# A gated conv-MLP with two more of its up-projection pairs per layer done in seven half products, and a new order of the products and of their weights' splits

## The chip, the cores and the metric

The kernel is one program on one core of a Trainium2 chip. The metric is the device time of one execution in microseconds (us). TensorE multiplies, ScalarE (ACT) and VectorE (DVE) work elementwise, GpSimd (POOL) issues some of the transfers, SyncE (SP) the others.

## What is computed

The reference is a decoder trunk of two layers on 512 tokens of width 1024. Layer 0 mixes tokens by a gated linear recurrence, layer 1 by an RWKV-7 recurrence. Behind each mixer stands the same channel mixer, and the change is in it alone:

```
h = rmsnorm(x, norm)
u = einsum('btd,df->btf', h, w_up)                 # 1024 -> 6144
gate = causal_dwconv(u[..., :3072], conv_w, conv_b)  # 3 taps
hid = gelu(gate) * u[..., 3072:]
x = x + einsum('btf,fd->btd', hid, w_down)         # 3072 -> 1024
```

## The kernel before

All of it is in float32. Each operand is split into two rounded parts, hi and lo (ACT casts hi, DVE subtracts to get lo), and a product is three matmuls: hi with hi, hi with lo, lo with hi (`mm3`).

The 3072 hidden columns of a channel mixer are worked off in twelve pairs, n = 0 to 11. A pair is 256 columns of the gate and the same 256 of the up part. There are two ways to do one.

- A pair of class `Whole` has four products G0, U0, G1, U1: gate or up, first or second half of the 1024 input rows. Each is 24 matmuls over 512 tokens.
- A pair of class `Halves` halves the tokens too and uses seven products instead of eight half-size ones, as Strassen and Winograd do: products 1 to 7 on sums of weights and on sums of tokens, each 24 matmuls over 256 tokens. Products 1, 6, 7 and 4 accumulate in this order into one PSUM bank (`accA`), products 5 and 3 into another (`accF`), product 2 into a third (`accD`). After 1, 6 and 7, ACT copies the bank `accA` out as it then stands, since the partial sums are needed one by one: `nc.scalar.copy(s[p], bank["A"])`, line 769. After 7, DVE adds bank `accF` to that copy (line 775).

The weights of a Halves pair are sums of blocks of `w_up`. Two of the sums are made by the transfer itself: SP fetches one block (line 166), and when it has landed POOL issues a second transfer that adds another block on top (line 168). A third sum is made by DVE (line 741), and when that one has been used, POOL adds one more block to it by a transfer (line 752), which makes the weights of product 3.

Every two pairs there is a projection down, `down`: four pieces of 24 matmuls, for pairs n - 3 and n - 2 (eight pieces, for the last four pairs, where n is 11). The program for n = 3, 5, 7, 9, 11 is: the products of pairs n - 1 and n up to product 7 of pair n; the first piece of the projection down; products 3 and 4 of pair n; the other pieces.

Pairs 3, 5, 7, 9, 11 of both layers are Halves, ten in all; pairs 0, 1, 2, 4, 6, 8, 10 are Whole. `products` runs through the list of products; `ahead` issues the splits of the weights of a Halves product two products before it is used.

What sets the order: the program is written in the order above, but a scheduler places the instructions of each engine within the limits of the data, so that TensorE can have matmuls of another product between two that depend on each other. Each engine then runs its list strictly in order. The split weights, the fetched blocks and the eight normalized inputs share one ring of 21 buffers of 4 KB for each partition (`N4`); while a channel mixer runs, 13 of them are left for weights, and a split or a fetch waits for the engine that last used its buffer.

## Time and profile before

| | |
|---|---|
| median of three runs | 1277.94 us (1277.94, 1279.1, 1277.94) |
| the profiled execution | 1279.1 us, span 1277.3 us |
| granted TensorE clock, mean | 0.998 |
| TensorE busy | 1256.0 us, 98% of the span |
| DVE, ACT, POOL busy | 929.2, 642.8, 131.1 us |
| channel mixer of layer 0 | about 155 to 541 us of the span |
| RWKV mixer | about 541 to 884 us |
| channel mixer of layer 1 | about 884 to 1250 us |

Start times are from the span's start. A matmul is listed with its modelled duration, which overlaps the next one's; what counts is the distance from start to start. In the chain that ended last, a line such as "PE accG L54 x24" is one product, and its second number is the time until the next product's start. L54, L94 and so on are lines of the kernel; `raw` is a fetched block of weights, `wh` and `wl`, `hi` and `lo` are split weights, `xs` and `xt` are the inputs and their sums, `acc` with a capital letter is a PSUM bank of an up product, plain `acc` one of the projection down.

### The profile page before, as it was taken

To read this page: it belongs to the slowest core of one execution; us is meant where nothing else is said; L and a number is where in the kernel's file an instruction comes from. 1 tells how busy PE (TensorE), PEld (TensorE's weight loads), DVE (VectorE), ACT (ScalarE), POOL (GpSimd) and SP (SyncE) were. 2 spreads that over 40 slices of the span, in tenths; PEclk is the share of its full clock that TensorE was granted. 3 is DMA by queue.
4 is the path that set the end of the run, shared out by engine and by line. 5 is a ranking of instruction groups with operands and counts; after the bars stand their busy time and mean duration, and the time that the engine had idled before them with its cause. 6 is when DMAs were issued, how large, how long until landed. Compare 5 with 4: busy or idle time off the path is not lost. (4 is left out here: it accounts for less than half of the span.)

```text
span 1277.3 us, 22409 instructions
## 1 busy us (share of the span) xinstructions
PE 1256.0 (98%) x9259; PEld 1067.4 (84%) x9259; DVE 929.2 (73%) x1412; ACT 642.8 (50%) x1006; POOL 131.1 (10%) x206
## 2 busy tenths in 40 slices
PE   9999999999999999999999898999999999999998
PEld 8777888989898989877778797778889898989896
DVE  5998678767676767789999967778776666666654
ACT  6797455434343434559845356545644334343442
POOL 3000001010101010010012145310010101000000
PEclk9999999999999999999999999999999999999999
DMA  7312335445454544413222122122345454545431
GB/s 228 109 53 97 98 119 114 158 106 167 97 175 89 181 83 137 141 57 110 67 75 68 35 63 85 50 94 83 127 88 181 83 182 83 182 83 182 98 133 66
DMA packets 117829, 141.37 MB, mean 111 GB/s; under 512 B 10138, under 2 KB 91748, under 8 KB 117600
## 3 DMA queue, kind: packets, MB, share of 16 engines
q1 hardware_dynamic: 100528, 122.44, 29.9%
q0 software_dynamic: 16624, 16.47, 8.3%
q8 instruction: 72, 1.18, 0.4%
q10 hardware_dynamic: 576, 1.05, 0.2%
q14 instruction: 29, 0.24, 0.1%
HBM read 135.41 MB, written 4.52 MB: 110 GB/s over the span
## 5 line engine op out<-in xcount | busy, mean ns | idle before, releaser
L97 DVE TENSOR_TENSOR wl<-raw,wh 128x1024 fp32r<-128x1024 f32 (+1 forms) x161 | 194.4, 1213 | 123.6 <-ACT wh L94 103.8
L94 ACT CAST wh<-raw 128x1024 fp32r<-128x1024 f32 (+1 forms) x161 | 165.9, 1043 | 179.8 <-PE acc L54 40.7
L54 PE MATMUL accU<-xs,wh 128*128 128x512 f32 x448 | 138.6, 391 | 0.0
L54 PE MATMUL accG<-xs,wh 128*128 128x512 f32 x448 | 138.6, 390 | 0.0
L54 PE MATMUL acc<-hid,wh 128*128 128x512 f32 x384 | 117.9, 389 | 0.0
L748 DVE TENSOR_TENSOR lo<-raw,hi 128x1024 fp32r<-128x1024 f32 x70 | 85.5, 1222 | 39.4 <-PE accU L54 32.0
L747 ACT CAST hi<-raw 128x1024 fp32r<-128x1024 f32 x70 | 73.7, 1054 | 60.4 <-PE accU L54 25.3
L54 PEld LDWEIGHTS accU<-xs,wh 128*128 128x128 f32 x448 | 83.7, 188 | 17.1
L54 PEld LDWEIGHTS accG<-xs,wh 128*128 128x128 f32 x448 | 83.7, 188 | 17.0
L54 PE MATMUL accU<-xs,wl 128*128 128x512 f32 x224 | 87.2, 389 | 0.0
L54 PE MATMUL accG<-xs,wl 128*128 128x512 f32 x224 | 87.2, 389 | 0.0
L54 PE MATMUL accA<-xt,hi 128*128 128x256 f32 x480 | 83.5, 277 | 0.0
L54 PEld LDWEIGHTS acc<-hid,wh 128*128 128x128 f32 x384 | 71.4, 188 | 14.3
L54 PE MATMUL acc<-xs,wh 128*128 128x512 f32 x256 | 80.9, 398 | 0.0
L694 DVE SCALAR_TENSOR_TENSOR cv<-gpad,pv,cv 128x512 f32<-128x512 f32 x96 | 69.1, 747 | 13.1 <-ACT cv L692 12.7
L848 PE MATMUL acc<-wh,hid 128*128 128x512 f32 (+1 forms) x200 | 76.2, 381 | 0.0
L849 PE MATMUL acc<-wl,hid 128*128 128x512 f32 (+1 forms) x200 | 76.1, 381 | 0.0
L847 PE MATMUL acc<-wh,hid 128*128 128x512 f32 (+1 forms) x200 | 76.1, 381 | 0.0
L54 PE MATMUL acc<-hid,wl 128*128 128x512 f32 x192 | 74.3, 389 | 0.0
L168 POOL DMA_DIRECT2D raw<-in_ffn_w_up_dram x20 | 25.7, 1285 | 469.8 <-DVE x L863 166.5
L54 PEld LDWEIGHTS accA<-xt,hi 128*128 128x128 f32 x480 | 72.6, 188 | 0.0
L54 PE MATMUL accA<-xt,lo 128*128 128x256 f32 x240 | 66.3, 276 | 0.0
(411 smaller groups left out, 2938.0 us busy)
## 6 DMA issues: line engine op xcount, KB each, us to landing
raw<-in_ffn_w_up_dram SPq DMA_DIRECT2D x106, 512.0 KB, 3.9
raw<-in_ffn_w_down_dram SPq DMA_DIRECT2D x48, 512.0 KB, 4.0
raw<-in_ffn_w_up_dram POOLq DMA_DIRECT2D x30, 512.0 KB, 5.7
raw<-in_rwkv_w_rkv_dram SPq DMA_DIRECT2D x24, 512.0 KB, 3.8
raw<-in_lru_w_in_dram SPq DMA_DIRECT2D x16, 512.0 KB, 4.0
raw<-in_lru_w_out_dram SPq DMA_DIRECT2D x8, 512.0 KB, 3.8
raw<-in_rwkv_w_out_dram SPq DMA_DIRECT2D x8, 512.0 KB, 3.8
xd<-x SPq DMA_DIRECT2D x8, 256.0 KB, 2.1
```

What stands on the lines that cost most here:

```text
L54: mm = lambda *a, **kw: self.nc.tensor.matmul(ps, *a, skip_group_check=more, **kw)
L94: put = (self.nc.vector.tensor_copy if dve else self.nc.scalar.copy)(hi, src)
L97: self.nc.vector.tensor_tensor(lo, src, hi.bitcast(F32), ALU.subtract)
L168: self.nc.gpsimd.dma_start(raw, more, accum_op=ALU.add)
L694: nc.vector.scalar_tensor_tensor(cv, pair.gp[:, e, j : j + T], cw(j), cv, ALU.mult, ALU.add)
L747: nc.scalar.copy(hi, f[p])
L748: tt(lo, f[p], hi.bitcast(F32), ALU.subtract)
L847: nc.tensor.matmul(ps, hh[:, s], wh[:, k, m], start=kk == 0, stop=False)
L848: nc.tensor.matmul(ps, hl[:, s], wh[:, k, m], start=False, stop=False)
L849: nc.tensor.matmul(ps, hh[:, s], wl[:, k, m], start=False, stop=kk == blocks - 1)
```

## The change

Pairs 6 and 10 of both layers become Halves, so that 14 of the 24 pairs are. The order of a Halves pair's products goes from 1, 5, 6, 2, 7, 3, 4 to 1, 2, 5, 6, 7, 3, 4, and the order in which its blocks are fetched follows. A new limit `cap` holds back the splits for the next pair while the projection down runs, until `prepare` lifts it in the second half of the projection; the fetches for a Halves pair that follows stand in the middle of the projection down (`fetch`), or, for an odd pair, behind the first product or product 5 of the pair before. The splits of the projection's weights are asked for after product 7 of odd pairs alone.

```
-HALVES = (3, 5, 7, 9, 11)
+HALVES = (3, 5, 6, 7, 9, 10, 11)
...
-for first, more in (((0, 0), None), ((1, 1), (1, 0)), ((0, 1), None), ((1, 0), (0, 0)), ((1, 1), None)):
+for first, more in (((0, 0), None), ((0, 1), None), ((1, 1), (1, 0)), ((1, 0), (0, 0)), ((1, 1), None)):
...
-order = ((1, 5, 6, 2, 7), (3, 4))
+order = ((1, 2, 5, 6, 7), (3, 4))
...
-    pair.f = dict(zip((1, 5, 2, 7), [self.loaded.pop(i + j) for j in range(4)]))
+    pair.f = dict(zip((1, 2, 5, 7), [self.loaded.pop(i + j) for j in range(4)]))
...
-    nc.gpsimd.dma_start(f[3], self.plan[i + 2][0], accum_op=ALU.add)
+    nc.gpsimd.dma_start(f[3], self.plan[i + 1][0], accum_op=ALU.add)
...
-    while made[0] < min(j, len(seq)):
+    while made[0] < min(j, cap[0]):
...
-    if p == "G0" and n + 1 in HALVES:
+    if p in ("G0", 5) and n % 2 == 0 and n + 1 in HALVES:
         self.weights_load(quads[n + 1] + 4)
...
-    if p == 7:
+    if p == 7 and n % 2:
         self.weights_split(behind[n] + 2)
...
+def fetch(n):
+    if n in HALVES:
+        self.weights_load(quads[n] + 4)
+def prepare():
+    cap[0] = len(seq)
+    ahead(at[0] + 2)
...
     products((n, 7))
+    cap[0] = seq.index((n, 4)) + 1
...
-    down(n, 2 * n - 6, 4 if n < 11 else 8, lambda: products((n, 4)), lambda: ahead(at[0] + 2))
+    down(n, 2 * n - 6, 4 if n < 11 else 8, lambda: products((n, 4)), lambda: fetch(n + 1), prepare)
```

What the scheduler made of it shows on TensorE between products 6 and 7. Both accumulate into `accA`. In pair 3 of layer 0, before, product 6 (weights `lo_2022`) was followed by product 2 into `accD`:

```order
L54 MATMUL accA<-xt,lo_2022 128x256
L54 MATMUL accA<-xt,hi_2021 128x256 x2
L54 MATMUL accA<-xt,lo_2022 128x256
L54 MATMUL accD<-xs_1412,hi_2053 128x256 x2
L54 MATMUL accD<-xs_1412,lo_2054 128x256
```

Now product 6 (`hi_2052`) is followed by four matmuls of the projection down (`acc_2189`), and then by product 7 (`hi_2086`):

```order
L54 MATMUL accA<-xt,hi_2052 128x256 x2
L54 MATMUL accA<-xt,lo_2053 128x256
L54 MATMUL acc_2189<-hid,wh_2179 128x512 x2
L54 MATMUL acc_2189<-hid,wl_2180 128x512
L54 MATMUL acc_2189<-hid,wh_2179 128x512
L54 MATMUL accA<-xt,hi_2086 128x256 x2
L54 MATMUL accA<-xt,lo_2087 128x256
```

So the 24 matmuls of product 2 that stood between the two writers of `accA` have become four of another kind. In the new Halves pair 6 the place between 6 (`hi_2960`) and 7 (`hi_2994`) holds two matmuls, the first of product 1 of pair 7:

```order
L54 MATMUL accA<-xt,hi_2960 128x256 x2
L54 MATMUL accA<-xt,lo_2961 128x256
L54 MATMUL accA<-xs_1262,hi_3095 128x256 x2
L54 MATMUL accA<-xt,hi_2994 128x256 x2
L54 MATMUL accA<-xt,lo_2995 128x256
```

Before, pair 6 was Whole, and its second and third products went into two different banks, one behind the other:

```order
L54 MATMUL accU<-xs_1317,wh_2920 128x512 x2
L54 MATMUL accU<-xs_1317,wl_2921 128x512
L54 MATMUL accG<-xs_1412,wh_2962 128x512 x2
L54 MATMUL accG<-xs_1412,wl_2963 128x512
L54 MATMUL accG<-xs_1431,wh_2962 128x512 x2
```

In pair 7, which follows a Halves pair, product 7 (`hi_3238`) stands directly behind product 6 (`hi_3204`); pair 11 behind pair 10 is the same, and layer 1 repeats all of it:

```order
L54 MATMUL accA<-xt,lo_3205 128x256
L54 MATMUL accA<-xt,hi_3204 128x256 x2
L54 MATMUL accA<-xt,lo_3205 128x256
L54 MATMUL accA<-xt,hi_3238 128x256 x2
L54 MATMUL accA<-xt,lo_3239 128x256
```

On ACT, in the pair 5 of before, the three copies out of `accA` (L769) stood with one or two casts between them:

```order
L769 COPY s<-accA 128x512
L747 CAST hi_2673<-raw_2610 128x1024
L769 COPY s<-accA 128x512
L94 CAST wh_2707<-raw_2705 128x1024
L94 CAST wh_2713<-raw_2711 128x1024
L769 COPY s<-accA 128x512
```

In the pair 6 of after, three casts stand between the copy behind product 1 and the one behind product 6: those of products 3 and 4 (`hi_3033`, `hi_3063`) and that of product 1 of the next pair (`hi_3095`):

```order
L769 COPY s<-accA 128x512
L747 CAST hi_3033<-raw_2850 128x1024
L747 CAST hi_3063<-raw_2992 128x1024
L747 CAST hi_3095<-raw_3023 128x1024
L769 COPY s<-accA 128x512
L747 CAST hi_3125<-raw_3025 128x1024
L769 COPY s<-accA 128x512
```

The copy that product 7 waits for has thus moved behind the cast of a weight block that pair 7 uses.

More of the change, by code (lines that the diff above doesn't have):

```diff
@@ L797, in ffn @@
             seq = [(n, p) for n in range(12) for part in kind(n).order for p in part]
-            made, at = [0], [0]
+            made, at, cap = [0], [0], [len(seq)]
             def ahead(j):
-                while made[0] < min(j, len(seq)):
+                while made[0] < min(j, cap[0]):
                     n, p = seq[made[0]]
@@ L824, in products, with down @@
                         return
-            def down(n, b0, blocks, between, then):
+            def down(n, b0, blocks, between, then, soon):
                 final = n == 11
@@ L854, in down @@
                                             finish(b, m, xtok[:, b, :], pool)
+                                if g and b == 1:
+                                    soon()
                             if not g and cs[0] == 0:
@@ L871, in hook @@
                                 then()
+                            elif g and c == pieces - 2:
+                                soon()
                         self.project(hids, ev, kb=blocks, join=2 if g else 1, rate=0.5 if final else 2, after=hook, x0=b0)
```

## The prediction

> **What bounds the kernel now.** I read the busy times first, then the chain of work that ended last, then a table by stage, and last the engines' own rows around one Halves pair.
>
> ```profile
> PE 1256.0 (98%) x9259; PEld 1067.4 (84%) x9259; DVE 929.2 (73%) x1412; ACT 642.8 (50%) x1006; POOL 131.1 (10%) x206
> ```
>
> TensorE works through 98% of the span. A busy PE is not always PE at its pace, so I look at the chain in the channel mixer of layer 1, where each line is one product and its second number the time to the next start:
>
> ```profile
> 933.53 5.44 PE accG L54 x24
> 938.97 5.44 PE accU L54 x24
> 944.41 5.44 PE accG L54 x24
> 949.85 5.44 PE accU L54 x24
> 955.29 2.87 PE accA L54 x24
> 958.16 2.74 PE accF L54 x24
> 960.90 2.72 PE accA L54 x24
> 963.62 2.86 PE accD L54 x24
> 966.48 2.74 PE accA L54 x24
> ...
> 974.68 2.87 PE accF L54 x24
> 977.55 2.74 PE accA L54 x24
> ...
> 1144.57 2.87 PE accA L54 x24
> ```
>
> A Whole pair is four lines of 5.44 us, 21.76 us. A Halves pair is seven, 2.87 + 2.74 + 2.72 + 2.86 + 2.74 + 2.87 + 2.74 = 19.54 us. One line begins where the last one ends: TensorE waits for nothing here. The table shows one period of two pairs with its projection down, for layers 1 and 0 (columns: busy us of PE, weight load, DVE, ACT, POOL, then clock, DMA share, GB/s):
>
> ```profile
> 955.29:1018.38 63.09, 63.09 (x362) 55.59 (x362) 39.86 (x47) 25.25 (x31) 3.82 (x3) 1.00 0.50 134
> 284.00:347.00 63.00, 63.00 (x361) 55.50 (x361) 41.60 (x52) 25.05 (x30) 3.81 (x3) 1.00 0.50 134
> ```
>
> DVE is idle for a third, ACT for more than half. So matmuls taken away shorten the time directly, and any wait on TensorE lengthens it directly.
>
> **The gain.** Four pairs go from 21.76 to 19.54 us: 4 x 2.22 = 8.9 us less.
>
> **The extra work beside it.** Each of these pairs gets three more casts on ACT and three more subtractions and one sum on DVE, three copies out of PSUM, and some 512-wide DVE operations. How densely these follow each other is in these rows:
>
> ```profile
> 203.46 1.21 DVE L748 TENSOR_TENSOR lo<-raw,hi 128x1024 fp32r<-128x1024 f32 x1
> 204.60 0.68 DVE L97 TENSOR_TENSOR hid<-s,hid 128x512 fp32r<-128x512 f32 x1
> 205.20 0.68 DVE L726 TENSOR_TENSOR s<-s,ge 128x512 f32<-128x512 f32 x1
> ```
>
> A wide DVE operation takes a slot of 1.14 us, a narrow one 0.60. Four wide ones and about three narrow ones are 6.4 us of DVE; with 39.9 to 41.6 in the table that is 46 to 48 of the 60.8 us that a period of two Halves pairs would last (2 x 19.54 + 4 x 5.44). ACT goes to about 30. Neither becomes the bound by its sum. SP gets one more fetch per pair, POOL three adding transfers where a Whole pair had none. Held-back splits (`cap`) and the earlier fetch cost nothing by themselves: the blocks of pair 6 are asked for once the first down piece has freed their buffers, some 17 us before they are used (two products and three pieces, 5.6 + 3 x 5.44 = 21.9 us, less a fetch of 3.9 and its cast); if that cover were gone, product 1 would wait.
>
> **The new wait, bare.** The old order had product 2 between 6 and 7; now 7 follows 6 at once. Both write bank `accA`, and 7 may not start before ACT has copied the bank. What such a copy costs is in these rows:
>
> ```profile
> 1146.72 1.05 ACT L747 CAST hi<-raw 128x1024 fp32r<-128x1024 f32 x1 [0.70 <-DVE lo L748]
> 1147.68 0.58 ACT L769 COPY s<-accA 128x512 f32<-128x512 f32 x1
> 1147.81 1.23 DVE L748 TENSOR_TENSOR lo<-raw,hi 128x1024 fp32r<-128x1024 f32 x1 [0.52 <-ACT hi L747]
> ...
> 1152.74 0.39 PE L54 MATMUL accD<-xs,hi 128*128 128x256 f32 x2
> 1152.94 0.59 ACT L769 COPY s<-accA 128x512 f32<-128x512 f32 x1 [3.73 <-PE accA L54]
> 1153.82 1.05 ACT L94 CAST wh<-raw 128x1024 fp32r<-128x1024 f32 x1 [0.29 <-DMA raw<-in_ffn_w_down_dram]
> 1154.89 1.23 DVE L97 TENSOR_TENSOR wl<-raw,wh 128x1024 fp32r<-128x1024 f32 x1 [4.43 <-ACT wh L94]
> ```
>
> The copy begins 0.20 us after the next product's first matmul and takes 0.59. An ACT cast lets the next instruction start after 0.96 us; DVE starts 0.04 us after the cast it needs. For the step from ACT to TensorE I take the nearest case, in the RWKV mixer:
>
> ```profile
> 639.84 1.05 ACT L94 CAST wh<-raw 128x1024 fp32r<-128x1024 f32 x1
> 640.93 0.50 PE L54 MATMUL acc<-mix,wh 128*128 128x512 f32 x1 [1.57 <-ACT wh L94]
> ```
>
> The cast ends at 640.89, the matmul starts 0.04 later and takes 0.50 instead of the usual 0.39, so 0.11 us more for a weight load that nothing hides. A bare gap is 0.20 + 0.59 + 0.04 + 0.11 = 0.94 us. The 0.11 may not arise, since here the weights were what was waited for; I take it and keep 0.83 as the lower end. On that point the Trainium skill (TensorE: Matmul & The Clock Gate, "Step-by-step: what each phase is for") says that weight loads are pulled ahead of matmuls in flight; by that rule each bare gap would be 0.83, and the sum below 0.9 us lower. The row here is of the other kind and can't decide it.
>
> **Where it is paid, pair by pair.**
>
> Pairs 3, 5 and 9 (six in two layers) follow a Whole pair. Four down matmuls stand in the gap, 4 x 5.44/24 = 0.91 us. They need the down weights early: their `lo` part was ready 11.55 us after product 1 of its pair (1154.89 + 1.23 less 1144.57), and the third of the four is due at 11.19 + 0.45 = 11.64 us. That just fits, since the fetch still waits for the second product. I book 0.05 each, 0.3 in all; nothing to 0.4 each are the ends.
>
> Pairs 7 and 11 (four) have nothing in the gap: 0.94 each, 3.8 in all, if ACT is free. Ahead of that copy ACT has two gelus, a cast and two casts of the hidden block, which I count to end 0.4 to 0.6 us early.
>
> Pairs 6 and 10 (four) have two matmuls, 0.24 us, but ACT is late there. I count from product 1 of pair 6: products end at 2.87, 5.73, 8.47 and 11.19 (1, 2, 5, 6). The ring of buffers orders the rest: `hi` of product 3 takes the buffer of the last product but one, `lo` of 3 and `hi` of 4 those of product 5, and the cast for pair 7 waits for `lo` of 4. So `lo` of 3 starts on DVE at 8.6 and holds it to 9.75, `lo` of 4 ends at 9.76 + 1.22 = 10.98, the cast for pair 7 runs from 11.02, and the copy of product 6 behind it starts at 11.98 and ends at 12.57. Product 7 starts at 12.57 + 0.04 + 0.11 = 12.72 instead of 11.43: 1.3 us. In layer 1, DVE adds the last down block before it splits product 6's weights (0.2 + 0.7 + 1.2 us after the pair's start), so POOL starts the transfer for product 3 at 2.1:
>
> ```profile
> L168 POOL DMA_DIRECT2D raw<-in_ffn_w_up_dram x20: 1258/1276/1378, 196.9 to 1188.9; - x20
> ...
> DMA to landing us min/median/max: 5.6/5.7/7.5
> ...
> L752 POOL DMA_DIRECT2D raw<-in_ffn_w_up_dram x10: 1261/1277/1301, 214.8 to 1200.1; - x10
> ...
> DMA to landing us min/median/max: 5.6/5.7/6.4
> ...
> raw<-in_ffn_w_up_dram SPq DMA_DIRECT2D x106, 512.0 KB, 3.9
> ```
>
> It lands at 7.85, the cast of product 3 ends at 8.9, and the same chain gives 13.1: 1.7 us. Two such pairs in each layer: 2 x 1.3 + 2 x 1.7 = 6.0 us.
>
> Behind product 7 of these four pairs stand six matmuls of pair 7, then ten of product 4, then product 3. Product 4 waits for the copy of 7 (0.20 + 0.59 after its end, against 0.72 of cover); product 3 waits for DVE, which first splits a block whose buffer product 7 frees, then adds bank F: 0.20 + 1.14 + 0.69 against 0.72 + 0.07 + 1.14 of cover. I book 0.2 each, 0.8 in all; 0 to 0.5 each are the ends.
>
> **The sum.** -8.9 + 0.3 + 3.8 + 6.0 + 0.8 = +2.0 us. Against the profiled execution (1279.1 us, 1.2 above the median) that is 1281.1; against the median, 1279.9. The RWKV mixer's instructions are also placed a little differently, since the scheduler sees another start, and TensorE has idle time there:
>
> ```profile
> 541.00:884.00 343.00, 331.33 (x4282) 272.50 (x4281) 284.94 (x521) 197.77 (x386) 73.60 (x142) 1.00 0.23 71
> ```
>
> Of 343.0 us it is busy for 331.3; I allow an eighth of the 11.7 idle, 1.5 us either way. A difference under 0.2% (2.6 us) can't be told from none here. With all lower ends (0.83 bare, nothing for the six and the 0.8, even pairs without the 0.11) the sum is -8.9 + 3.3 + 5.6 = 0.0, with all upper ones +2.0 + 2.1 + 1.2 = +5.3.
>
> **The rivals.**
>
> *The gaps are mostly covered.* The scheduler put two matmuls into the gaps of pairs 6 and 10, as if the copy were on time; if the buffers came free earlier than I count, those gaps would cost 0.94 - 0.24 = 0.7 us, the 0.8 would go, and the sum would be -8.9 + 0.3 + 3.8 + 2.8 = -2.0, with gaps of 0.83 about -2.9: 1275.0 to 1276. Against it: the chain from the end of product 5 (cast, subtraction, cast, copy) is made of durations above and has no slack.
>
> *A transfer comes late, and the kernel is clearly slower.* POOL adds the second block for product 5 of pair 7 once SP's fetch has landed. SP issues that at about 3.5 (behind product 1's buffers and two fetches), it lands 3.9 later, and 5.7 more make 13.1 to 14. On DVE the sum that needs it stands ahead of the addition of bank F that product 3 of pair 6 waits for. The split between the two starts when product 7 has ended (15.4 + 0.2), so with a slot of 1.14 for the sum the transfer may land at 14.4 at the latest; at the 7.5 us of the slowest adding transfer it lands at 15 to 16, about 1.2 us late in each of four pairs: +2.0 + 4.8 = +6.8, 1284.7. For it speaks that eight transfers of 512 KB meet in 20 us there; against it that most took 5.7.
>
> *The clock drops.* After a gap the chip once granted half the clock (columns: busy us of PE, clock, DMA share, GB/s), though not after the gap at 640.93:
>
> ```profile
> 793.50:794.00 0.50, 0.00 (x0) 1.00 1.05 426
> ...
> 796.50:797.00 0.50, 0.17 (x4) 0.82 0.00 0
> 797.50:798.00 0.50, 0.50 (x13) 0.50 0.12 33
> ...
> 799.50:800.00 0.50, 0.50 (x17) 0.50 1.13 135
> 800.00:800.50 0.50, 0.50 (x5) 0.76 0.71 102
> ...
> 640.00:645.00 5.00, 4.07 (x17) 3.06 (x18) 4.83 (x11) 2.79 (x3) 0.00 (x0) 1.00 0.16 61
> ```
>
> That is some 3.4 us at half speed, 1.7 us lost. Four even pairs with that would add 6.8 us: 1286.7. TensorE had little work from 793.5 to 796.9; my gaps are 1.3 us between dense products, shorter than the harmless one of 1.57. The Trainium skill warns of it in the same page ("A second HAM failure mode: psum-queue depth-cycling"): short idle times between matmul groups can make the clock swing. Its table asks for no idle gap over about 3 us ("Why this matters for your kernels"), which the quoted gap at 640.93 agrees with.
>
> **How the numbers follow.** My sum holds with 60%, the covered gaps with 17%, the late transfer with 17%, the clock with 6%. In my own case a little under two thirds lies within 0.2% and the rest above. Faster by over 0.2% comes from the covered gaps: 12%. Slower: 17 + 6 + 20 = 43%. The same: 45%. The range from 1275.8 to 1285.0 takes in the covered gaps, all ends of my terms and the late transfer, and leaves out the clock and a part of each tail. My own case by itself is 1278 to 1283.
>
> **What would show it.** Right: in the chain of the changed kernel the products of a Halves pair keep 2.72 to 2.87 us, and TensorE shows idle time ended by the copy at line 769, about 0.9 us in pairs 7 and 11 and 1.3 to 1.7 in 6 and 10. Periods of pairs 6 and 7 with their projection take 60.8 us plus about 2.5. Wrong: no idle time before product 7; or idle time before product 3 of pair 6 that ends with DVE, which had waited for an adding transfer; or a clock under 1.00 in these stretches; or a change in the RWKV mixer larger than 1.5 us.

## The result, and the profile after

The changed kernel takes 1313.79 us (median of four, 1313.4 to 1314.05), against 1278.18 before: 1.0275 times as long, 95% interval 1.0263 to 1.0287. The prediction had 1279.9 us, 1275.8 to 1285.0 as its range. It was wrong by 34 us.

The first lines of the page of the changed kernel, busy times and the fetches of `w_up`:

```profile
PE 1260.8 (96%) x9547; PEld 1080.3 (82%) x9547; DVE 954.5 (73%) x1440; ACT 657.9 (50%) x1030; POOL 146.3 (11%) x218
...
raw<-in_ffn_w_up_dram SPq DMA_DIRECT2D x110, 512.0 KB, 3.8
...
raw<-in_ffn_w_up_dram POOLq DMA_DIRECT2D x42, 512.0 KB, 5.8
```

DVE and ACT have hardly more to do than before, and the median landing times, 3.8 and 5.8 us, are near the 3.9 and 5.7 of before. Nothing here explains 34 us. The waits of TensorE do (engine and operation, what released it: us in total, times, longest):

```profile
PE accA L54 <- ACT hi L747: 12.9, 4, 6.3
PE accF L54 <- DVE s L775: 6.0, 2, 3.6
PE acc L54 <- ACT wh L94: 4.5, 3, 2.2
PE accA L54 <- ACT s L769: 4.4, 4, 1.5
```

The wait that I had booked, on the copy at line 769, is the last of the four. The two above all are on a cast (747) and on the addition of bank F (775). Where they lie is seen by stage: first the couple of pairs 6 and 7 with its projection in the kernel before, and the stretch from the rest of the last projection of layer 0 to layer 1; then the same in the changed kernel, with the couples 10/11 up to product 4 of pair 11. Columns as in the prediction's table.

```profile
327.21:390.30 63.09, 63.09 (x361) 55.59 (x360) 41.70 (x51) 25.07 (x30) 3.81 (x3) 1.00 0.50 134
500.15:884.08 383.93, 372.26 (x4462) 306.27 (x4461) 319.78 (x566) 220.91 (x417) 73.60 (x142) 1.00 0.25 77
```

```profile
328.42:397.30 68.88, 63.68 (x434) 58.96 (x432) 44.36 (x56) 28.23 (x35) 5.09 (x4) 0.98 0.60 161
460.72:511.44 50.72, 45.85 (x362) 43.94 (x361) 30.97 (x38) 18.97 (x24) 5.09 (x4) 1.00 0.71 171
511.44:902.54 391.10, 373.35 (x4463) 306.13 (x4462) 325.11 (x570) 223.14 (x419) 73.47 (x142) 1.00 0.24 76
1078.67:1150.12 71.45, 63.97 (x433) 59.65 (x432) 43.29 (x52) 28.38 (x36) 6.47 (x5) 0.95 0.62 160
1213.63:1266.89 53.26, 47.45 (x362) 45.94 (x360) 30.53 (x34) 21.17 (x27) 5.71 (x5) 0.94 0.69 179
```

With nothing lost, a couple 6/7 would last 63.09 - 2.22 = 60.87 us, a couple 10/11 up to there 46.76 - 2.22 = 44.54 (the 46.76 is the same piece of before). So the four couples of two Halves pairs lose 8.0 and 6.2 us in layer 0, 10.6 and 8.7 in layer 1, 33.5 together. I call this the loss of a couple below. The account of the spans (1311.9 against 1277.3, 34.6 more): -8.9 gained, +33.5 in the couples, +2.0 in the six odd Halves pairs behind a Whole (0.30 to 0.41 each), +7.2 in the stretch to layer 1 (391.10 against 383.93), +0.8 in small shifts at both ends. The sum of the prediction was +2.0.

**What happens in layer 1, pair 6.** The adding transfer for product 3 and the four plain fetches for pair 7, each by its line:

```profile
L752 POOL DMA_DIRECT2D raw<-in_ffn_w_up_dram x1: 1283/1283/1283, 1081.6 to 1081.6; - x1
...
DMA to landing us min/median/max: 9.9/9.9/9.9
```

```profile
L166 SPq DMA_DIRECT2D raw<-in_ffn_w_up_dram x4: 367/408/892, 1081.6 to 1084.5; - x4
...
DMA to landing us min/median/max: 4.1/9.6/10.0
```

At 1081.6, three us into pair 6, POOL starts the add for product 3 (line 752) and SP, in the next three us, the four plain fetches for pair 7. From 1086 to 1091 us the DMA engines are full (share 1.10). The add lands after 9.9 us instead of 5.7; the first fetch still lands after 4.1 us, the others after up to 10.0 instead of 3.9. Now the order of the lists, on ACT and on TensorE:

```profile
1091.56 1.99 ACT L747 CAST hi<-raw 128x1024 fp32r<-128x1024 f32 x2 [9.23 <-DMA raw<-in_ffn_w_up_dram]
1095.21 1.04 ACT L747 CAST hi<-raw 128x1024 fp32r<-128x1024 f32 x1 [1.66 <-DVE lo L748]
1096.16 0.58 ACT L769 COPY s<-accA 128x512 f32<-128x512 f32 x1
...
1096.31 0.80 PE L54 MATMUL accA<-xs,hi 128*128 128x256 f32 x2 [6.26 <-ACT hi L747]
```

ACT stands 9.23 us at the cast for product 3, which waits for the add. Behind it stand the cast for product 4, the first cast for pair 7 and the copy of bank A. TensorE has two matmuls of pair 7's product 1 ahead of product 7 and waits 6.26 us for their weights, and all of this for a product 3 that is not due yet.

**What happens in layer 0.** Here POOL starts the add for product 3 earlier, and it lands in 5.9 us. The adds for pair 7 are late (DVE's list and the matmul that waited for it):

```profile
346.89 1.23 DVE L741 TENSOR_TENSOR raw<-raw,raw 128x1024 f32<-128x1024 f32 x1 [4.96 <-DMA raw<-in_ffn_w_up_dram]
348.03 1.22 DVE L748 TENSOR_TENSOR lo<-raw,hi 128x1024 fp32r<-128x1024 f32 x1
349.16 0.68 DVE L775 TENSOR_TENSOR s<-s,accF 128x512 f32<-128x512 f32 x1
...
349.90 0.71 PE L54 MATMUL accF<-xs,hi 128*128 128x256 f32 x2 [3.59 <-DVE s L775]
```

That is the prediction's second rival as it stands there: the sum at 741 stands ahead of the addition of bank F. Only it ends 3.6 us late instead of 1.2.

**And the clock.** Stretches of half a microsecond (the last three columns are clock, DMA share, GB/s), the first behind a wait of 2.43 us, the others in and behind longer ones:

```profile
481.00:481.50 0.50, 0.46 (x4) 0.47 (x5) 0.50 (x1) 0.00 (x0) 0.00 (x0) 1.00 0.00 0
350.50:351.00 0.50, 0.50 (x4) 0.50 (x4) 0.50 (x2) 0.00 (x0) 0.00 (x0) 0.50 0.00 0
1094.00:1094.50 0.50, 0.00 (x0) 0.00 (x0) 0.50 (x1) 0.00 (x0) 0.50 (x1) 0.63 0.01 4
1227.00:1227.50 0.50, 0.00 (x0) 0.00 (x0) 0.41 (x2) 0.04 (x1) 0.16 (x1) 0.75 0.44 137
```

Behind three of the four waits TensorE runs at half the clock for a while. In layer 0 product 3 takes 4.47 us from start to start instead of 2.87, so 1.6 us of the 8.0 are the clock. In layer 1 TensorE worked at half the clock for 4.6 and 4.3 us behind the two waits, which by the same reckoning makes about 2.3 us of the 10.6 and 2.1 of the 8.7 (an estimate from the clock's changes in the trace).

### The profile page after: what moved, and what is told of

Its sections match the earlier page's. It is cut to its first block, busy times and chain, and to the rows that moved or that the text cites. A ratio compares the mean times of both kernels' runs of the same rounds, so it can differ in the third digit from the quotient of the medians.

```text
span 1311.9 us, 23103 instructions
## 1 busy us (share of the span) xinstructions
PE 1260.8 (96%) x9547; PEld 1080.3 (82%) x9547; DVE 954.5 (73%) x1440; ACT 657.9 (50%) x1030; POOL 146.3 (11%) x218
## 3 DMA queue, kind: packets, MB, share of 16 engines
q0 software_dynamic: 22960, 22.76, 11.2%
## 4 chain that ended last, share of the span: by engine, by line
PE 37%; DVE 7%; ACT 4%; issue 2%; DMA 2%; POOL 1%; SPq 0%; POOLq 0%; ACTq 0%; DVEq 0%
PE acc L54 6%; PE accA L54 4%; PE accU L54 4%; PE accG L54 4%; PE acc L849 3%; PE acc L847 3%; PE acc L848 3%; PE accF L54 2%; DMA raw<-in_ffn_w_up_dram 2%; DVE X L1323 1%; DVE wl L97 1%; PE accD L54 1%; DVE DA L1321 1%; PE s L1437 1%; DMA raw<-in_ffn_w_down_dram 1%
## 5 line engine op out<-in xcount | busy, mean ns | idle before, releaser
L747 ACT CAST hi<-raw 128x1024 fp32r<-128x1024 f32 x98 | 102.6, 1050 | 143.4 <-DMA raw<-in_ffn_w_up_dram 39.8
L748 DVE TENSOR_TENSOR lo<-raw,hi 128x1024 fp32r<-128x1024 f32 x98 | 119.6, 1222 | 66.4 <-ACT hi L747 35.7
L54 PE MATMUL accA<-xt,hi 128*128 128x256 f32 x672 | 122.3, 284 | 4.4 <-ACT s L769 4.4
L54 PEld LDWEIGHTS accA<-xt,hi 128*128 128x128 f32 x672 | 105.2, 193 | 6.8 <-ACT s L769 6.3
L54 PE MATMUL accU<-xs,wh 128*128 128x512 f32 x320 | 99.2, 391 | 0.0
L54 PE MATMUL accG<-xs,wh 128*128 128x512 f32 x320 | 99.2, 391 | 0.0
L54 PE MATMUL accA<-xt,lo 128*128 128x256 f32 x336 | 94.5, 281 | 0.0
L54 PEld LDWEIGHTS accU<-xs,wh 128*128 128x128 f32 x320 | 59.6, 188 | 12.1
L54 PEld LDWEIGHTS accA<-xt,lo 128*128 128x128 f32 x336 | 64.9, 193 | 0.0
L54 PE MATMUL accU<-xs,wl 128*128 128x512 f32 x160 | 62.4, 390 | 0.0
```

The source lines that it names most:

```text
L54: mm = lambda *a, **kw: self.nc.tensor.matmul(ps, *a, skip_group_check=more, **kw)
L747: nc.scalar.copy(hi, f[p])
L748: tt(lo, f[p], hi.bitcast(F32), ALU.subtract)
```

## The experiments

Theory A: transfers that meet land late, and TensorE waits for them through the order of ACT's and DVE's lists. Theory B: the new order of products and the place of instructions cost it, the transfers little. This table sums up all runs. Losses are of the couples, in us, from TensorE's start times in each trace; the last column is the stretch from the rest of layer 0's last projection to layer 1. In e3 the even pairs begin up to 2.6 us inside the projection ahead, which counts as loss here, and its trace is of its slowest execution (1321.6 us).

| run | median us | 6/7, 10/11 of layer 0 | 6/7, 10/11 of layer 1 | sum | stretch |
|---|---|---|---|---|---|
| before | 1278 | - | - | - | 383.9 |
| changed | 1313.8 | 8.0, 6.2 | 10.6, 8.7 | 33.5 | 391.1 |
| e1 ten pairs | 1282.9 | - | - | - | 383.4 |
| e2 old order | 1295.7 | 4.9, 7.6 | 4.5, 3.9 | 20.8 | 388.1 |
| e3 kernel before, fourteen pairs | 1314.9 | 10.0, 10.1 | 14.2, 11.9 | 46.2 | 393.3 |
| e4 half of the couples' adds left out | 1295.7 | 2.7, 4.2 | 2.9, 3.6 | 13.4 | 391.3 |
| e5 plain instead of adds | 1301.1 | 3.6, 3.7 | 7.1, 4.3 | 18.8 | 391.6 |
| e6 no add for 3 | 1301.6 | 3.9, 4.5 | 8.3, 6.0 | 22.7 | 390.7 |
| e7 pair 10 Whole | 1293.1 | 8.5, - | 9.9, - | 18.4 | 381.5 |
| e8 sums on DVE, old order | 1289.0 | 3.2, 3.2 | 1.9, 1.8 | 10.2 | 391.5 |
| e9 DVE order | 1335.3 | 10.5, 8.4 | 15.8, 15.7 | 50.4 | 393.8 |
| e10 DVE order, no add for 3 | 1323.9 | 10.7, 9.1 | 11.5, 9.8 | 41.0 | 393.7 |
| e11 e8, pair 10 of layer 0 Whole | 1278.0 | 3.2, - | 1.9, 1.8 | 6.9 | 381.7 |
| e12 e11, product 1 earlier | 1277.1 | 2.5, - | 1.8, 1.8 | 6.1 | 381.8 |
| e13 ACT order | 1314.1 | 3.4, 7.6 | 10.4, 11.2 | 32.6 | 391.8 |
| e14 all three orders | 1305.9 | 8.7, 4.3 | 7.0, 4.9 | 25.0 | 391.8 |
| e15 e12, layer 1 alone | 1278.0 | - | 1.8, 1.8 | 3.6 | 382.2 |

**e1: the ten old pairs with all other edits.**

```
-HALVES = (3, 5, 6, 7, 9, 10, 11)
+HALVES = (3, 5, 7, 9, 11)
```

> The changed kernel with the old ten Halves pairs (3, 5, 7, 9, 11 in each layer) and every other edit kept: the new product order, the later splits, the earlier fetch. No Halves pair follows another here. Theory A (transfers that meet): four fetches and one adding transfer fall into some 5 us after the start of pairs 6 and 10, land after 6.5 to 10 us instead of 3.9 and 5.7, and TensorE waits for them through the order of ACT and DVE; without pairs 6 and 10 that is gone, and what is left is the new order after a Whole pair, 0.3 us in each of ten pairs as the chain of the changed kernel shows for pairs 3, 5 and 9: 1278.2 + 3 = 1281 us. Theory B (the new order itself and where ACT and DVE instructions stand): then this kernel should lose much of it too, 1290 us or more. The 7.2 us that the stretch from the last projection of layer 0 to the start of layer 1 lost: if they come with the edits of fetch and splits they are here too, and the time is about 1288; if they come from pairs 10 and 11, they are gone.

1282.93 us, 1.0031 times before (1.0020 to 1.0043). The edits without the couples cost 5 us: 4.0 in the ten pairs (0.17 to 0.52 each), most of the rest ahead of the first of them. The stretch to layer 1 is as before. So the time goes where two Halves pairs stand side by side.

**e2: the old order of products, fourteen pairs.**

```
-order = ((1, 2, 5, 6, 7), (3, 4))
+order = ((1, 5, 6, 2, 7), (3, 4))
```

> The changed kernel with fourteen Halves pairs, but the products in the old order 1, 5, 6, 2, 7 (and the blocks of a pair asked for in the old order). Theory A: the same transfers meet in the same 5 us, and the block for product 5 of pair 7 is needed even earlier; the gaps before product 7 are covered by product 2, so about 4 x 1.4 + 6 x 0.3 = 7 us go, but most of the 25 us of waits on transfers stays: 1300 to 1312 us. Theory B: with the order the loss goes too, and the gain of 8.9 us shows: below 1280 us.

1295.74 us, ratio 1.0129 (1.0112 to 1.0145): below A's range, far above B's. The order is worth 12.7 us in the couples, 2.0 in the six odd pairs, which lose nothing here, and 3.0 in the stretch; 20.8 stay in the couples with it. So Theory B has a large part too.

**e3: the kernel before with fourteen pairs and little else.**

```
-HALVES = (3, 5, 7, 9, 11)
+HALVES = (3, 5, 6, 7, 9, 10, 11)
...
-    if p == 7:
+    if p == 7 and n % 2:
```

> The kernel before with fourteen Halves pairs and nothing else of the change (splits for the projection down asked for after product 7 of odd pairs alone, as they must be): old order, no early fetch of a pair behind a Halves pair, so the blocks of pairs 7 and 11 are asked for only when the weights of their product 1 are prepared. Theory A: the fetches come together and later than in the changed kernel, so the waits are as long or longer: 1310 us or more. Theory B: the old order has no gap, so the gain of 8.9 us shows in part: 1270 to 1280 us.

1314.9 us (1311.05 to 1321.63), ratio 1.0288 (1.0252 to 1.0323), as A had it. The old order alone does not carry fourteen pairs.

**e4: without three of the six adding transfers of each couple,** those behind which TensorE was seen to wait. The adds for products 5 and 7 of pairs 6 and 10 and for product 3 of pairs 7 and 11 stay.

```
-plan.append((a(*first), 4, True, more and a(*more)))
+plan.append((a(*first), 4, True, more and n not in (7, 11) and a(*more) or None))
...
-if p == 6:
+if p == 6 and pair.n % 2:
     nc.gpsimd.dma_start(f[3], self.plan[i + 1][0], accum_op=ALU.add)
```

> The changed kernel without the adding transfers in the couples 6/7 and 10/11: the second block is not added for products 5 and 7 of pairs 7 and 11, nor for product 3 of pairs 6 and 10 (so those weights are incomplete); every fetch, cast, sum and product stays. Theory A: no cast and no sum waits for an adding transfer, and the plain fetches land sooner. The gap before product 7 of pairs 6 and 10 falls from 1.1 to 6.4 us to about 1, the wait before product 3 (3.6 and 2.4 us) and the half clock go; the four couples lose about 2.4 to 3 us each instead of 6.2 to 10.6: 1313.8 - 33.5 + 11 = about 1291 us. Theory B: the waits are set by buffers and by the order on ACT and DVE, with the transfers only last in line by little: less than 8 us go, 1306 us or more.

1295.74 us, ratio 1.0137 (1.0118 to 1.0155); the couples lose 13.4. Its waits:

```profile
PE accA L54 <- ACT s L769: 5.2, 4, 2.1
PE acc L54 <- ACT wh L94: 4.5, 3, 2.2
PE accA L54 <- ACT hi L747: 3.8, 4, 0.9
```

The wait on bank F is gone, that on the cast is 0.9 us at most. Twenty of the 33.5 us hang on these adding transfers. What is left, 13.4, is near the 10.6 that the prediction had for the couples (3.8 + 6.0 + 0.8).

**e5: the same transfers, plain.**

```
-self.nc.gpsimd.dma_start(raw, more, accum_op=ALU.add)
+self.nc.gpsimd.dma_start(raw, more)
...
-nc.gpsimd.dma_start(f[3], self.plan[i + 1][0], accum_op=ALU.add)
+nc.gpsimd.dma_start(f[3], self.plan[i + 1][0])
```

> The changed kernel with every adding transfer of POOL turned into a plain one of the same block at the same place (it overwrites instead of adding, so these weights are incomplete). Number, bytes, queue and order of the transfers stay. Theory A1 (adding is what is slow: with an adding transfer under way the DMA engines are full at 165 to 200 GB/s, without one they move 300 to 385): the plain ones land after about 4 us also when they meet others, and the couples fall to near the kernel without adds, 13 to 18 us lost instead of 33.5: 1293 to 1299 us. Theory A2 (too many transfers at once, whatever they do): the five that meet still land after 6 to 10 us, and the time stays above 1308 us.

1301.05 us, ratio 1.0172 (1.0157 to 1.0188), couples 18.8: between the two, nearer A1. The transfer for product 3 in pair 6 of layer 1, which took 9.9 us as an add:

```profile
L752 POOL DMA_DIRECT2D raw<-in_ffn_w_up_dram x1: 760/760/760, 1077.3 to 1077.3; - x1
...
DMA to landing us min/median/max: 7.3/7.3/7.3
```

In layer 0, where it starts 1.5 us ahead of the fetches, the plain one took 4.2. So both count: of the 20 us that the adds cost, 14.7 go when the adding goes, and about 5.4 (18.8 less 13.4) when the transfers go too. The split is rough, since this edit takes the adding from all six transfers of a couple and e4 leaves three of them.

**e6: no add for product 3 in pairs 6 and 10.** The second edit of e4 alone.

> The changed kernel without the adding transfer for product 3 of the even Halves pairs (6 and 10) alone; those of pairs 7 and 11 stay (so product 3's weights of pairs 6 and 10 are incomplete). If the gap of 4.8 to 6.3 us before product 7 in layer 1 comes from this transfer alone (it took 8.8 and 9.9 us to land, and ACT's next casts stood behind the cast that waited for it), it falls to about 1 us with the half clock behind it: 10 to 12 us less. In layer 0 the waits of 3.6 and 2.4 us before product 3 come from the adds for pairs 7 and 11; they stay, or lose 1 to 2 us with the lighter traffic. In all 1298 to 1304 us. Rival: with the gap gone, TensorE in layer 1 reaches product 3 earlier and waits there for the sum behind the adds of pair 7, as layer 0 does: only 5 to 7 us less, 1306 to 1309 us.

1301.57 us, ratio 1.0169 (1.0149 to 1.0189). The wait before product 7 of the even pairs falls to 0.95 us in layer 1 too, as expected; the rival came true beside it:

```profile
PE accF L54 <- DVE s L775: 7.5, 4, 3.0
```

Layer 1 now waits before product 3, which it did not before. In layer 0 that wait fell from 3.6 and 2.4 to 1.0, since the lighter traffic let the adds for pair 7 land sooner.

**e7: pair 10 a Whole pair.** `HALVES = (3, 5, 6, 7, 9, 11)`.

> The changed kernel with pair 10 as a Whole pair again (twelve Halves pairs: 3, 5, 6, 7, 9, 11). By the account of the changed kernel's chain the two couples 6/7 stay at 8.0 and 10.6 us of loss, the couples 10/11 lose nothing, eight odd pairs behind a Whole cost 0.3 each: 1278 - 4.4 + 18.6 + 2.5 + 0.8 = 1295.5 us, if the 7.2 us lost between the last products of layer 0 and the start of layer 1 come from the couple 10/11 that ends layer 0. If they come from a state that the couple 6/7 or the whole layer leaves, they stay: 1303 us.

1293.06 us, ratio 1.0106 (1.0091 to 1.0121). The couples 6/7 lose 8.5 and 9.9, close to the 8.0 and 10.6 of the changed kernel, and the stretch to layer 1 is back at 381.5: its 7.2 us come from the couple that ends layer 0.

**e8: sums on DVE in place of every adding transfer, old order.** The second blocks are in the buffers anyway, as blocks of other products; the blocks are fetched for products 1, 5, 7, 2 and 3 in turn.

```
+if p == 5:
+    tt(f[5], f[5], f[7], ALU.add)
+    tt(f[7], f[7], f[1], ALU.add)
 if p == 6:
     tt(f[1], f[5], f[1], ALU.add)
...
+if p == 2:
+    tt(f[3], f[3], f[2], ALU.add)
```

> Fourteen Halves pairs in the old product order, and no adding transfer at all: the blocks are fetched plainly and added by DVE out of blocks that are in the buffers anyway (product 5's from the blocks for 5 and 7, product 7's from those of 7 and 1, product 3's from those of 6 and 2). Everything is computed. DVE pays three sums of 1.14 us a pair. Theory A: with no add to wait for and with the gap before product 7 covered by product 2, the couples lose about 1 to 2 us each; 1278 - 8.9 + 6 + 4 to 7 in the mixer = 1279 to 1282 us, under 1278 if the mixer's loss goes too. Rival: DVE, at 46 to 48 of 60.8 us in a couple plus 6.8 for the sums, now comes late itself, and the splits behind the sums make TensorE wait: 1290 us or more.

1288.97 us, ratio 1.0078 (1.0061 to 1.0095), above what A gave, though the couples lose only 10.2; the longest wait of TensorE in them is 0.8 us. I had the mixer wrong again: the stretch is at 391.5, 7.6 more than before.

**e9: the late sum held back on DVE.**

```
+with tc.issue_after(mark[0].ins):   # product 3's addition, pair 6 or 10
     pairs[n].weights(p)             # p = 5, 6 of pair 7 or 11
```

> The changed kernel, all transfers as they are, with one thing held on DVE: the splits and the sum for products 5 and 6 of pairs 7 and 11, which need the late block, are queued behind product 3's addition of the pair before, as the program text has them (the scheduler had put the sum ahead of the addition of bank F). Theory: in layer 0 TensorE's wait of 3.6 and 2.4 us before product 3 is the order on DVE alone, since the product that needs the late block comes 9 us later; it goes, with the half clock behind it, and the couples of layer 0 fall from 8.0 and 6.2 us to about 2.7 and 4.2 (what is left without adds). In layer 1 the wait before product 7 stands behind product 3's add and stays: 10.6 and 8.7. In all 7.3 us less: 1306 to 1307 us. Rival: the late block is late for pair 7 itself, and the wait only moves on to its products 5 or 6: less than 3 us gained, 1311 us or more.

1335.27 us, ratio 1.0445 (1.0430 to 1.0461): 21 us worse than the changed kernel. The wait before product 3 did go. But the sum now ran at 352.4 instead of 346.9, the add of pair 7's own product 3 started later and met the fetches for the projection down, and ACT and TensorE show the next place:

```profile
365.56 1.04 ACT L747 CAST hi<-raw 128x1024 fp32r<-128x1024 f32 x1 [5.72 <-DMA raw<-in_ffn_w_up_dram]
366.51 0.58 ACT L769 COPY s<-accA 128x512 f32<-128x512 f32 x1
...
367.14 0.80 PE L54 MATMUL accA<-xt,hi 128*128 128x256 f32 x2 [5.90 <-ACT s L769]
```

The same pattern as in pair 6 of layer 1, now in pair 7: a cast that waits for an add stands ahead of the copy of bank A. My theory that the order on DVE alone was at fault in layer 0 fell with this.

**e10: the same without the add for product 3 of pairs 6 and 10.**

> The same, and the adding transfer for product 3 of pairs 6 and 10 left out as well (so product 3's weights of these pairs are incomplete); the adds for pairs 7 and 11 stay. If the two waits, on product 3's add through ACT and on the sum that stands ahead on DVE, are the whole of what the adding transfers cost, the four couples lose what they lose without any adds, 13.4 us together instead of 33.5: 1293 to 1296 us. If there is a third cost of the adds for pairs 7 and 11, the couples stay above 18 us: 1299 us or more.

1323.92 us, ratio 1.0355 (1.0340 to 1.0371). There is a third cost, and it is that of e9: the waits before product 7 of the odd pairs, 4.6 to 7.0 us, stay. The changed kernel does not have it, its waits there are 0.7 to 1.5 us, so it came with the order held on DVE.

**e11: e8 with pair 10 of layer 0 Whole.**

> The kernel of the DVE sums in the old order, with pair 10 of layer 0 a Whole pair again (thirteen Halves pairs). The stretch from the last products of layer 0 to layer 1 took 391 us in every kernel whose pairs 10 and 11 are both Halves there, 381 to 384 where pair 10 is Whole. If that is the cause, this kernel loses 3.2 us of its couple less, gains 2.2 less, and gets 7 to 10 us back in the mixer: 1289.0 - 1.0 - 8 = about 1280 us. Rival: the mixer's time hangs on the whole order ahead of it in no simple way, and stays near 391: 1288 us.

1278.0 us, ratio 0.9993 (0.9984 to 1.0003). Eleven us less than e8, more than I expected, nearly all of it in the stretch to layer 1 (e8, then e11):

```profile
502.85:894.37 391.52, 372.15 (x4462) 304.62 (x4461) 326.11 (x571) 223.17 (x419) 74.30 (x142) 1.00 0.24 76
```

```profile
501.19:882.93 381.74, 370.87 (x4462) 304.88 (x4461) 319.81 (x566) 220.86 (x417) 74.99 (x142) 1.00 0.24 77
```

TensorE has the same 4462 matmuls and DVE five instructions more in e8; TensorE idles 19.4 us in e8 and 10.9 in e11.

**e12: e11, with product 1 of pairs 7 and 11 ahead of products 3 and 4 of the pair before.**

> As the last one, and product 1 of pairs 7 and 11 stands between product 7 and products 3 and 4 of the pair before it, so that the copy of bank A and the addition of bank F have 2.9 us of matmuls beside them. The gaps of 0.44 us and what goes with them (0.1 for the reload) in three couples go: 1 to 2 us below the last kernel, 1278 to 1279 us. Rival: the next pair's weights are then needed 5 us earlier, and the splits and sums for them are late: 1283 us or more.

1277.08 us, ratio 0.9991 (0.9982 to 1.0001). The couple of layer 0 loses 2.5 instead of 3.2, those of layer 1 no more than in e11, so the rival did not come true.

**e13: the cast for product 3 held back on ACT, in pairs 6 and 10.**

```
+with tc.issue_after(mark[6].ins):   # the copy after product 6
     pairs[n].weights(p)             # p = 3
```

> The changed kernel, all transfers as they are, with one thing held on ACT: the cast for product 3 of pairs 6 and 10, which waits for the adding transfer, is queued behind the copy of bank A after product 6 instead of ahead of it and of pair 7's first cast. If the 4.8 and 6.3 us before product 7 in layer 1 are the order on ACT alone (product 3 itself is due 3.4 us later and could still meet its block), they fall to about 1 us with the half clock behind them, and the couples of layer 1 fall from 10.6 and 8.7 to about 4 us: 1302 us. If the run of dependent transfers is late as a whole (block for product 3 landed, then the fetches and adds for pair 7), the wait moves to the next instruction that hangs on it, product 4 or 3 of the same pair, as it moved when the sum was held back on DVE: 3 us gained or less in each couple of layer 1, none in layer 0: 1307 to 1313 us.

1314.13 us, ratio 1.0283 (1.0266 to 1.0300): no change in all. (The edit also asks for the weights of product 3 one product later.) The wait before product 7 of pair 6 in layer 1 is 0.67 us now, and pair 7 has this:

```profile
1115.83 0.80 PE L54 MATMUL accA<-xt,hi 128*128 128x256 f32 x2 [6.37 <-ACT s L769]
```

Against what I expected, layer 0 changed too: couple 6/7 fell from 8.0 to 3.4, its wait on bank F gone, and couple 10/11 rose from 6.2 to 7.6.

**e14: all three places mended at once,** e9 and e13 together, e13's also for pairs 7 and 11.

> The changed kernel, all transfers as they are, with both held orders together and on both pairs of a couple: on DVE the splits and the sum for products 5 and 6 of pairs 7 and 11 behind product 3's addition of the pair before, on ACT the cast for product 3 behind the copy of product 6, in pairs 6, 7, 10 and 11. These are the three places at which TensorE was seen to wait behind an instruction that waits for an adding transfer. If the cost of the adds is order alone, it is gone now, and the couples lose about 3 to 4 us each: 1294 to 1300 us. If the blocks are late for the pair's work itself, the wait has a fourth place to go to (the casts of the weights for the projection down, which stand behind the cast for product 3 of pairs 7 and 11) and the time stays above 1308 us.

1305.93 us, ratio 1.0211 (1.0192 to 1.0230), couples 25.0. Between the two: these three orders gain 8.5 of the 20 us and not the other 11.6. But order is not used up by them. In layer 0 TensorE now waits one copy later, before product 4 of pair 7, and the half clock comes with it (from 366.5 to 373.3 us):

```profile
364.59 1.99 ACT L747 CAST hi<-raw 128x1024 fp32r<-128x1024 f32 x2 [3.32 <-DMA raw<-in_ffn_w_up_dram]
366.49 0.58 ACT L769 COPY s<-accA 128x512 f32<-128x512 f32 x1
...
367.12 0.80 PE L54 MATMUL accA<-xt,hi 128*128 128x256 f32 x2 [2.79 <-ACT s L769]
```

The cast for product 3, which waits for its add, stands ahead of the copy after product 7 here. So how the 11.6 us part between late data and order that is left stays open.

**e15: even Halves pairs in layer 1 alone,** otherwise e12.

> DVE sums in place of the adding transfers, old order, product 1 of the next pair ahead of products 3 and 4, and even Halves pairs in layer 1 alone (twelve Halves pairs in all). In the run with pair 6 of layer 0 as well, the couple there lost 2.5 us against 2.2 gained, those of layer 1 about 1.8 each. So 0.3 us below that run: 1276.8 us against 1278.5, if the mixer takes the 382 us it took there; at the 383.9 of the kernel before it comes out at 1278.5, no faster.

1277.96 us, ratio 0.9991 (0.9982 to 1.0000). Level with the kernel before or a tenth of a percent faster; the stretch took 382.2.

## Why the prediction was wrong, point by point

**The step that failed: the durations of the transfers.** The sum and the rival "a transfer comes late" took 3.9 us for a fetch and 5.7 for an add, from medians over the whole kernel, with the slowest add, 7.5, as the upper end. Those rows came mostly from places where the transfers have room. In the couples, an add and four fetches are asked for within five us. The fetches took 5.6 to 10.0 us (but for the first of layer 1, 4.1 in pair 6), the adds for product 3 in layer 1 8.8 and 9.9. The prediction named the eight transfers that meet and then priced them as if alone. In layer 1 its own chain for the even pairs (transfer, cast, subtraction, cast, copy) was the right one. It gave product 7 a start 13.1 us after that of product 1, with POOL starting at 2.1 and 5.7 for the transfer. POOL started at 2.9, 0.8 us behind the end of DVE's split, and the transfer took 9.9: 13.1 + 0.8 + 4.2 = 18.1. The trace has 1096.90 - 1078.67 = 18.23. In layer 0, where the add for product 3 took 5.9, it gave a start of product 7 12.72 us after that of product 1, and the trace has 341.21 - 328.42 = 12.79.

The trace is 32.6 us above the sum (+34.6 against +2.0). Of these, 20.1 hang on the adding transfers that e4 leaves out, 2.8 are the rest of the couples (13.4 against the 10.6 booked), 1.7 the six odd pairs, 7.2 the stretch to layer 1 and 0.8 the ends. Three of the prediction's own signs of being wrong came: the wait before product 3 that ends with DVE, the clock, and the mixer.

**The rival had the mechanism and not the size.** The sum at 741 ahead of bank F: 1.2 us late by the prediction, 3.6 and 2.4 in layer 0. Its fetch was to land 7.4 us after the pair's start and its add at 13.1 to 14; POOL could start it only at 340.2, 11.8 after the start, and the sum ran at 18.5. I gave this rival 17%, and 1.2 us in each of four pairs. A late transfer acted in a second place too, through ACT in layer 1, where the prediction saw only its own 1.7 us.

**The clock was priced as if apart from the late transfer.** I compared it with gaps of 1.3 us. All 18 waits of TensorE of 3.6 us or more in the kept traces brought the half clock with them, so the two rivals were one case, not two.

**The RWKV stretch.** An allowance of 1.5 us either way; it lost 7.2. That stretch takes 388 to 394 us in every run whose pairs 10 and 11 of layer 0 are both Halves, 381 to 384 in all others (e7, e11, e12, e15, e1). The cause is shown to be that couple, not how it acts. A part is seen in the changed kernel: TensorE waits 1.95 us for weights of the last projection, whose cast on ACT (523.73) stands behind a cast of the next mixer's weights that waits 1.31 us for DVE; the rest stays open.

**The six odd pairs behind a Whole.** 0.05 us each, nothing to 0.4 as ends; they took 0.30 to 0.41. The step that I had let "just fit" did not: the third down matmul waits for its `lo` part, from DVE's line 97. In pair 3 of layer 0 the copy of bank A, which the gap was about, ended at 235.38, ahead of the start of product 7 at 235.80; what came late is this weight load:

```profile
235.23 0.19 PEld L54 LDWEIGHTS acc<-hid,wl 128*128 128x128 f32 x1 [0.44 <-DVE wl L97]
```

The load starts 0.64 us after the first of the four matmuls (234.59) instead of 0.45, and 0.11 more go as in a bare gap: 0.30.

**Right.** The gain, 2.22 us a pair: the products keep 2.72 to 2.88 us. The bare gap of pair 7, 0.94 us: in layer 0 products 6 and 7 take 6.40 us from start to start of what follows, against 2.72 + 2.74, so 0.94. The trace has the first matmul behind that gap:

```profile
367.05 0.51 PE L54 MATMUL accA<-xt,hi 128*128 128x256 f32 x2 [0.67 <-ACT s L769]
...
367.05 0.30 PEld L54 LDWEIGHTS accA<-xt,hi 128*128 128x128 f32 x2 [0.87 <-ACT s L769]
```

It takes 0.51 instead of 0.39, the 0.11 of a weight load that nothing hides: the load, too, began only when the copy had ended. The rule of the Trainium skill quoted in the prediction (TensorE: Matmul & The Clock Gate, "Step-by-step: what each phase is for") is about loads pulled ahead of matmuls in flight; in this gap none was in flight, and the 0.83 that the prediction drew from the rule did not come. In the other three odd pairs of a couple the copy itself came later, and TensorE idled 1.0 to 1.5 us instead of 0.67.

**Where the lead went.** In the kernel before, the blocks of a Halves pair are fetched during the Whole pair ahead of it, and nothing is due before they land. In a couple there is no Whole pair in between, and the buffers come free only as pair 6 uses its weights, so the fetches start two to three us into pair 6. Reordering ACT and DVE mostly changes who waits: with one list mended, the couples lost 50.4 (e9) and 32.6 us (e13), with all three 25.0, against 33.5. Leaving out half of the adds takes 20 us out (e4). The order of products has its own large share, and the two overlap: the old order alone takes 12.7 us out of the couples (33.5 to 20.8, e2), and sums on DVE, which had the time, take out another 10.6 with it (20.8 to 10.2, e8). No variant is faster than the kernel before by more than its interval. Whether more buffers would help was not tried.

## What to carry to other kernels

A median landing time belongs to the traffic in which it was measured. Before a transfer is booked as hidden, list what else the change asks for in the same five microseconds, and count with every instruction queued behind the waiting one on each in-order engine. Even the slowest add of the kernel before, 7.5 us, was no upper end here: two took 8.8 and 9.9. When mending one list only moves the wait (e9, e13), the order of that list is not the whole cause; leaving the transfer out (e4) measures what hangs on it. Sums that an engine with time to spare can make from blocks already on the chip save that wait without a transfer.

## What the runs showed of the hardware

A transfer of 512 KB that adds took 5.6 to 5.9 us by itself or with a lead of 1.5 us on the fetches, a plain one from POOL 4.1 to 4.2 (e5), one from SP 3.5 to 3.9. Issued together with four fetches (pair 6 of layer 1), the first took 9.9 and the second 7.3. The fetch that SP issued at 1081.6 beside the add landed after 4.1 us. Three transfers asked for at 1081.6, 1082.1 and 1083.1 landed within 1.6 us of each other, at 1091.5, 1091.7 and 1093.1. The Trainium skill (DMA: Bandwidth & Descriptors, "SWDGE vs HWDGE vs iDMA") says that each DMA engine takes its queues in turns; such landing times fit that, but no run here shows the turns themselves.

The clock fell after no fixed idle time. It stayed full through 2.43 us of idle time (row at 481.00), fell 2.2 us into another wait (at 1227.25, idle since 1225.0), 4.1 us into a third (at 1094.1, idle since 1090.0). And once it fell after far less, behind small matmuls and a wait of 0.87 us:

```profile
561.08 1.58 PE L339 MATMUL rbc<-ident,rs 128*128 128x128 f32 x8 [0.87 <-POOL rs L335]
```

```profile
561.50:562.00 0.50, 0.50 (x5) 0.50 (x4) 0.00 (x0) 0.00 (x0) 0.00 (x0) 0.65 0.00 0
```

There it stayed at half until 565.1, 3.4 us. What is fixed is when it can change: in each of the seventeen kept traces all changes of the clock lie whole steps of 3.41 us apart (in the changed kernel at 350.02, 353.44, 561.65, 565.06, 1094.13, 1100.95, 1227.25 and 1234.07). So it also counts where a wait falls on this grid: the same wait of 1.95 us before the last projection of layer 0 brought the half clock in e10 and not in the changed kernel. The Trainium skill (TensorE: Matmul & The Clock Gate, "HAM oscillation — how this bites in real kernels") warns of idle gaps over about 3.4 us; the waits of 3.6 us and more agree, those of 1.95 and 0.87 us do not.
